# Output projection of a DeltaNet/mLSTM block on one core: two equal seven-product DeltaNet blocks, the last 512 mLSTM columns behind them, and two 512-column mLSTM blocks in the DeltaNet drain

## The chip, the core and the metric

One Trainium2 chip, one of its cores. The time is that of one launch, in microseconds (us) on the device. The kernel before was run three times: 2253.58, 2257.16 and 2258.36, median 2257.16. The profile is of one further execution, which took 2254.1 us. Engines are named as in the profile: PE is TensorE (PEld its weight loads), DVE VectorE, ACT ScalarE, POOL GpSimd, SP SyncE, which issues DMAs. `SPq` and `ACTq` are the queues in which SyncE and ScalarE issue DMAs.

## The reference

One decoder block on 512 rows of 2048 columns, in float32:

```python
u = _rmsnorm(h, norm_w)
proj = jnp.matmul(u, w_in.astype(jnp.float32))
...
h_a = h_a * jax.nn.sigmoid(ml_o) * jax.nn.silu(ml_z)     # mLSTM branch, 512 x 2048
...
h_b = _merge_heads(h_b) * jax.nn.silu(dn_z)              # DeltaNet branch, 512 x 2048
...
y_a = jnp.matmul(h_a, w_out[:ML_WIDTH])
y_b = jnp.matmul(h_b, w_out[ML_WIDTH:])
return jax.nn.sigmoid(gate_a) * y_a + jax.nn.sigmoid(gate_b) * y_b
```

`h + y` then passes a final RMSNorm with the weight `final_norm_w`. The change touches only the last part: the two products with `w_out`, the gates, the residual and the final norm.

## The kernel before, in words

**Number format.** A float32 operand is split into a high part `hi` (ScalarE, `split_hi`, L135) and the rest `lo` (VectorE, `split_lo`, L138). Every product of two tiles is three matmuls: hi x hi, hi x lo, lo x hi. One row tile is P = 128 rows; NC = 4 of them make the 512 rows. KT = 16 tiles of 128 make the 2048 of the inner dimension, KH = 8 pairs of them. NO = 512 is a wide column block, NB = 256 a narrow one.

**Order of the work.** TensorE runs its instructions in the order in which the program writes them. The side work is made of generators: `start(gen, wait)` puts one on the list `active`, and each `tick()`, called between groups of matmuls, advances those that are due, so that their instructions are written at that place. For the engines other than TensorE a list scheduler orders what has been written, by priority: `urgent(n)` and `tc.high_priority` move an instruction ahead, `behind(eng)` puts it after the newest weight split on that engine ("A" ScalarE, "V" VectorE). Weight tiles pass one ring, `wr` of NRAW = 4 slots, and `wh`, `wl` of NSPL = 4 slots each; `plan` lists them in the order of use, and `prepare` loads up to RAHEAD = 4 and splits up to SAHEAD = 3 tiles ahead of the one in use. Other tiles use `wr` slots too: gate tiles `ty`, h tiles `hr`, and the `b21` below. Tiles of one tag get their slots in the order in which the program allocates them; a pool that is opened after another was closed gets its memory when the last use of the closed pool's tiles is over.

**Drain.** The last DeltaNet chains (dn_back, dn_chain, travel) run as generators beside four narrow mLSTM output blocks (loop from L1281; `proj_tm`, 16 ticks each): block b computes columns 256 b to 256 b + 255 of `h_a @ w_out[:2048]`, gates them with `tgn`, adds half of that to x and stores y_d. After each block `close()` (L1268) looks whether `active` is empty; if so it closes the drain's pools (wks, with the pool wk), opens the pool sb2 (ring `wr3` of three slots, scratch `t13` of one buffer, `s4`, `X2`) and sa2 (`su`), and starts `h_sums`.

**h sums.** `h_sums` (from L1237) loads the eight pairs of DeltaNet h tiles (`hs`, in `wr3`), forms four sums per pair into a `t13` tile (`hsum`, L1256 to L1259) and splits them with `split_scaled` (L1217 on ScalarE, L1218 on VectorE). They are the left operands of the seven products.

**Wide mLSTM blocks** (loop from L1521): columns 1024 to 1535 (nb = 2) and 1536 to 2047 (nb = 3), 192 matmuls of 512 columns each, 12 per k tile and two ticks per k tile. At the end of a block four gated evacuations (L1568), then the generator `store_y`: for each row tile a load of x, the operation of L1538 with `behind("V")`, a store to y_d. Beside the second one run `load_h` (DeltaNet h, split into `uh`, `ul` over the mLSTM h) and, from its tick 22, `lead`: three loads of quads and the preparation of the first.

**DeltaNet output.** `seven_stage` computes `h_b @ w_out[2048:]` in two blocks of 1024 columns (c1 and c2 = c1 + 512) by seven products in place of eight, on halves of the inner dimension, rows and columns. A *quad* is one pair of k tiles: three 256 KB loads into `wr3` (L527), sums of weights (`prep_sums`, L550, L551, L562) and splits (`prep_sums`, `prep_pair`). Group A has 4 products of 8 quads (192 matmuls), B has 3 (144). A stores its sum `ts` to DRAM (t2_d), and B reads it back. `sink_y` holds what the finished products turn into: gate tiles `ty` (L1316), gated (L1321), added to y_d by an accumulating GpSimd DMA.

**The last of the two blocks is special** (`final_y`, from L1356): its group B is cut into 24 single pieces, its own loads `b21` (L513) take `wr` slots, GpSimd subtracts eight times (L554) and issues the stores, and the final norm is written into a table `beside` by piece: reading y_d back (`known`), gates (`times`, L1399), additions (`plus`, L1406), squares (L1410), the norm weight (`weigh`, L1421, GpSimd), the factor (L1426 to L1428) and the scaled output (by_act L1432, by_dve L1438 and L1440). KLAST = 4 pieces are done row tile by row tile at the end.

Of the kernel before, what the change touches and what calls it, by code (L numbers as in the profile page):

```python
# [15 lines left out]
P = 128  # L16
S = 512
# [10 lines left out]
YNARROW = 4  # L28
# [3 lines left out]
KLAST = 4  # L32
# [23 lines left out]
def hybrid_body(  # L56
# [95 lines left out]
    plan += [("n", b * NB, k) for b in range(YNARROW) for k in range(0, KT, KP)]  # L152
    plan += [("o", nb * NO, k) for nb in range(YNARROW * NB // NO, D // NO) for k in range(KT)]
# [4 lines left out]
    def load_raw():  # L158
        kind, c, k = plan[len(raws)]
        if kind == "m":  # L160

            qk = w_in[k * P:(k + KP) * P, ML_Q:ML_V].rearrange("(k p) (a n) -> p k a n", p=P, a=2)[:, :, :, c * P:(c + 1) * P]
            src, nk, n = None, KP, NB
        elif kind in "in":
            src, nk, n = (w_in if kind == "i" else w_out)[k * P:(k + KP) * P, c:c + NB], KP, NB
        else:
            src, nk, n = w_out[k * P:(k + 1) * P, c:c + NO], 1, NO
# [89 lines left out]

    def proj_tm(col0, kind="i"):
        ps = [psj.tile([P, 2, NB], F32, tag="pj", name="pjt") for _ in range(2)]
        for kt0 in range(0, KT, KP):  # L260
            hi, lo = next_w(kind, col0, kt0)
            for c in range(NC):
                for k in range(KP):
                    kt = kt0 + k
                    o = ps[c // 2][:, c % 2, :]
                    tsl = slice(c * P, (c + 1) * P)
                    T.matmul(o, uh[:, kt, tsl], hi[:, k, :], start=(kt == 0 and c % 2 == 0), stop=False,
                             skip_group_check=True)
                    T.matmul(o, uh[:, kt, tsl], lo[:, k, :], start=False, stop=False, skip_group_check=True)
                    T.matmul(o, ul[:, kt, tsl], hi[:, k, :], start=False, stop=(kt == KT - 1),  # L270
                             skip_group_check=True)
                if c % 2:
                    tick()
        return ps

# [218 lines left out]
    def seven_stage(sbp, su, s4, X, t2_d, w_, k0, blocks, sinks, hook, final=None):  # L494
# [5 lines left out]
                 for g in ("A" if final and b == len(blocks) - 1 else "AB") for i in range(KH)]  # L500
        rawq, partq, b21 = [], {}, {}

        def in_final(b):
            return final is not None and b == len(blocks) - 1

        def load_b21(q):

            if q < len(quads) and in_final(quads[q][3]):
                _, c1, c2, b, g, i = quads[q]
                k2 = slice((k0 + 2 * i + 1) * P, (k0 + 2 * i + 2) * P)  # L510
                with tc.high_priority(offset=2 * PRIO):
                    b21[q] = wp.tile([P, NO], F32, tag="wr", name="b21", bufs=NRAW)
                    nc.sync.dma_start(b21[q], w_[k2, c1:c1 + NO])  # L513
# [25 lines left out]
        def prep_sums(q):  # L539
# [5 lines left out]
            with tc.high_priority(offset=2 * PRIO):  # L545
                ts = wp.tile([P, 1, NO], F32, tag="tg", name="ts", bufs=3)
                if g == "A":
# [5 lines left out]
                    if in_final(b):  # L553
                        G.tensor_tensor(out=b21[q], in0=b21[q], in1=ts[:, 0, :], op=ALU.subtract)  # L554
                        G.dma_start(t2_d[b % 2, i], b21[q])
                        load_b21(q + 1)
                    else:
                        nc.scalar.dma_start(t2_d[b % 2, i], ts[:, 0, :])
# [30 lines left out]
        def seven(n0, kind, c1, c2):  # L589
# [5 lines left out]
            if in_final(n0 // (2 * KH)):  # L595
                fin = final(c1, c2, m1, m5, m7, LHS["B"], split, t2_d[(n0 // (2 * KH)) % 2])
# [14 lines left out]
            if in_final(n0 // (2 * KH)):  # L611
                for n in range(KH - 2):
                    prep_sums(n0 + n + 1)
# [991 lines left out]
```

## Time and profile before

| | us |
|---|---|
| median of the runs (3) | 2257.16 (2253.58 to 2258.36) |
| the profiled execution | 2254.1 |
| its span, in which all instructions lie | 2252.3 |
| TensorE busy | 2171.1 (96%) |
| VectorE busy | 1699.0 (75%) |
| ScalarE busy | 956.4 (42%) |
| GpSimd busy | 298.6 (13%) |
| granted TensorE clock, mean | 0.99 |

The profile is one execution. A view groups instructions by line, engine, operation and tile; `L604` is line 604 of the kernel, `out<-in` the tiles by the program's names, `x16` a count. Times on a timeline count from the start of the span. In a waits view, `A <- B: 6.0, 1, 6.0` means that instruction A's engine stood idle for 6.0 us, once, 6.0 at most, and that B ended last. "PEclk" is the granted TensorE clock as a share of full speed. A busy share over the whole span mixes stages with different limits; what follows looks at the last 410 us alone.

### The profile page before, as it was taken

To read this page: it belongs to the slowest core of one execution; us is meant where nothing else is said; L and a number is where in the kernel's file an instruction comes from. 1 tells how busy PE (TensorE), PEld (TensorE's weight loads), DVE (VectorE), ACT (ScalarE), POOL (GpSimd) and SP (SyncE) were. 2 spreads that over 40 slices of the span, in tenths; PEclk is the share of its full clock that TensorE was granted. 3 is DMA by queue.
4 is the path that set the end of the run, shared out by engine and by line. 5 is a ranking of instruction groups with operands and counts; after the bars stand their busy time and mean duration, and the time that the engine had idled before them with its cause. 6 is when DMAs were issued, how large, how long until landed. Compare 5 with 4: busy or idle time off the path is not lost. (4 is left out here: it accounts for less than half of the span.)

```text
span 2252.3 us, 32412 instructions
## 1 busy us (share of the span) xinstructions
PE 2171.1 (96%) x10976; PEld 1797.4 (80%) x10976; DVE 1699.0 (75%) x2953; ACT 956.4 (42%) x1834; POOL 298.6 (13%) x362
## 2 busy tenths in 40 slices
PE   7999999999999999999999999999999998999986
PEld 5878778778788888888878887888888888987765
DVE  5788788778877777876789877777767685477777
ACT  5444444445444443444443433443444443243334
POOL 0320000000000000000322522222222211000124
PEclk9999999999999999999999999999999999999998
DMA  5456666667666776685776865767566665588686
GB/s 159 134 164 199 203 191 211 205 192 231 213 215 213 236 227 183 221 260 182 185 180 165 194 154 141 161 157 160 144 157 150 160 171 166 153 264 257 208 238 243
DMA packets 536264, 430.61 MB, mean 191 GB/s; under 512 B 241697, under 2 KB 403714, under 8 KB 536098
## 3 DMA queue, kind: packets, MB, share of 16 engines
q1 hardware_dynamic: 435682, 361.35, 56.7%
q10 hardware_dynamic: 98624, 63.00, 8.9%
q0 software_dynamic: 1792, 4.20, 0.9%
q8 instruction: 86, 1.41, 0.3%
q14 instruction: 80, 0.66, 0.1%
HBM read 340.27 MB, written 88.15 MB: 190 GB/s over the span
## 5 line engine op out<-in xcount | busy, mean ns | idle before, releaser
L135 ACT CAST wh<-wr 128x512 fp32r<-128x512 f32 (+1 forms) x560 | 389.9, 698 | 524.9 <-PE pj L253 244.8
L138 DVE TENSOR_TENSOR wl<-wr,wh 128x512 fp32r<-128x512 f32 (+1 forms) x560 | 470.0, 842 | 154.2 <-ACT wh L135 145.4
L252 PE MATMUL pj<-uh,wh 128*128 128x512 f32 x1024 | 428.6, 419 | 2.8 <-ACT yp L816 2.8
L254 PE MATMUL pj<-uh,wl 128*128 128x512 f32 x1024 | 400.8, 391 | 0.0
L253 PE MATMUL pj<-ul,wh 128*128 128x512 f32 x1024 | 399.9, 391 | 0.0
L605 PE MATMUL ps<-wl,uh 128*128 128x512 f32 x640 | 252.4, 394 | 5.8 <-DVE wl L138 5.7
L604 PE MATMUL ps<-wh,uh 128*128 128x512 f32 x640 | 251.2, 393 | 5.8 <-DVE X L664 4.1
L606 PE MATMUL ps<-wh,ul 128*128 128x512 f32 x640 | 249.8, 390 | 0.0
L135 ACT CAST wh<-t 128x1024 fp32r<-128x1024 f32 x112 | 117.9, 1053 | 267.4 <-PE ps L606 116.6
L135 ACT CAST wh<-ts 128x512 fp32r<-128x512 f32 x216 | 133.3, 617 | 231.0 <-DVE ts L562 180.8
L254 PEld LDWEIGHTS pj<-uh,wl 128*128 128x128 f32 x1024 | 192.5, 188 | 43.1
L605 PE MATMUL ps<-wl,suh 128*128 128x512 f32 x576 | 224.5, 390 | 1.7 <-DVE wl L138 1.7
L604 PE MATMUL ps<-wh,suh 128*128 128x512 f32 x576 | 224.8, 390 | 0.9 <-ACT qk L363 0.5
L606 PE MATMUL ps<-wh,sul 128*128 128x512 f32 x576 | 224.4, 390 | 0.0
L252 PEld LDWEIGHTS pj<-uh,wh 128*128 128x128 f32 x1024 | 193.5, 189 | 37.7 <-ACT yp L816 3.2
L253 PEld LDWEIGHTS pj<-ul,wh 128*128 128x128 f32 x1024 | 193.5, 189 | 32.8
L138 DVE TENSOR_TENSOR wl<-t,wh 128x1024 fp32r<-128x1024 f32 x112 | 141.0, 1259 | 50.3 <-ACT wh L135 49.8
L138 DVE TENSOR_TENSOR wl<-ts,wh 128x512 fp32r<-128x512 f32 x216 | 151.1, 703 | 33.6 <-ACT wh L135 33.6
L605 PEld LDWEIGHTS ps<-wl,uh 128*128 128x128 f32 x640 | 120.6, 188 | 39.0 <-DVE wl L138 15.1
L604 PEld LDWEIGHTS ps<-wh,uh 128*128 128x128 f32 x640 | 120.7, 189 | 35.9 <-DVE X L664 8.9
L550 DVE TENSOR_TENSOR t<-wr 128x1024 f32<-128x1024 f32 x112 | 137.2, 1225 | 7.4 <-DMA wr<-in_w_in_dram 6.9
L562 DVE TENSOR_TENSOR ts<-wr 128x512 f32<-128x512 f32 x104 | 71.7, 690 | 92.8 <-DMA wr<-t_d 73.9
(320 smaller groups left out, 3714.3 us busy)
## 6 DMA issues: line engine op xcount, KB each, us to landing
wr<-in_w_in_dram SPq DMA_DIRECT2D x704, 256.0 KB, 3.7
wr<-in_w_out_dram SPq DMA_DIRECT2D x144, 256.0 KB, 4.3
t_d<-ts ACTq DMA_DIRECT2D x96, 256.0 KB, 4.1
wr<-t_d SPq DMA_DIRECT2D x96, 256.0 KB, 4.0
wr<-in_w_in_dram SPq DMA_DIRECT2D x64, 128.0 KB, 2.9
xt<-in_x_dram SPq DMA_DIRECT2D x8, 512.0 KB, 7.1
tg_d<-X ACTq DMA_DIRECT2D x16, 256.0 KB, 5.5
tg_d<-to ACTq DMA_DIRECT2D x16, 256.0 KB, 5.0
```

The source lines that it names most:

```text
L135: newest["A"] = A.copy(hi, src).ins
L138: newest["V"] = V.tensor_tensor(out=lo, in0=src, in1=hi.bitcast(F32), op=ALU.subtract).ins
L252: T.matmul(ps[j], hi[:, k, wsl], uh[:, kt, :], start=(kt == 0), stop=False)
L253: T.matmul(ps[j], hi[:, k, wsl], ul[:, kt, :], start=False, stop=False)
L254: T.matmul(ps[j], lo[:, k, wsl], uh[:, kt, :], start=False, stop=(kt == KT - 1))
L550: V.tensor_tensor(out=t13, in0=r[:, 1:3, :], in1=r[:, 0:2, :], op=ALU.subtract)
L562: V.tensor_tensor(out=ts[:, 0, :], in0=r[:, 0, :], in1=r[:, 2, :], op=ALU.subtract)
L604: T.matmul(ps[t], ah, hi, start=(g == "A" and i == 0), stop=False, skip_group_check=True)
L605: T.matmul(ps[t], ah, lo, start=False, stop=False, skip_group_check=True)
L606: T.matmul(ps[t], al, hi, start=False, stop=(i == KH - 1), skip_group_check=True)
```

## The change

1. **Drain.** The four narrow blocks (YNARROW = 4, `proj_tm`, plan kind "n") are gone. In their place `wide_block` computes columns 0 to 511 and 512 to 1023 (YDRAIN = 2), with three pj banks and one wk bank each and with gate tiles `tgs` in the drain's pool wk (tags "ke" and "vn"). `close()` is called after each k tile. A third call of `wide_block` computes columns 1024 to 1535, with `load_h`, `lead` and gate tiles in X2, as the old second wide block did for the last columns.
2. **DeltaNet output.** Both blocks of 1024 columns now run the same two groups. `final_y`, the parts of `seven_stage` that serve it, `b21` and GpSimd's subtractions are gone. The last block's sink is `sink_last`: it closes the pool of `su` once group A is over, opens a pool with hf, fw and jk, adds the gated products to hf on GpSimd (`plus`) after reading y_d and x into hf (`known`), and starts `load_hm`.
3. **The last 512 mLSTM columns** (1536 to 2047) come behind them as `last_block`. `load_hm` loads the mLSTM h again, k tile by k tile, into a ring of its own ("hmr", three slots) and splits it over the DeltaNet h during group B and the block itself, in the order LAST (even k tiles first). The weights of the last KLAST = 6 k tiles have slots in `wr3`, `w2` and the ring; they are multiplied row tile by row tile, and behind each row tile stands `done_c`: gate, residual, square, factor, scaling, store. Squares (ScalarE) and `weigh` (GpSimd) of the first 1536 columns run beside the block.

The diff, cut to its core (the removed `final_y` and `proj_tm` are left out):

```diff
-YNARROW = 4
+YDRAIN = 2
...
-KLAST = 4
+KLAST = 6
...
-    plan += [("n", b * NB, k) for b in range(YNARROW) for k in range(0, KT, KP)]
-    plan += [("o", nb * NO, k) for nb in range(YNARROW * NB // NO, D // NO) for k in range(KT)]
+    plan += [("o", nb * NO, k) for nb in range(D // NO - 1) for k in range(KT)]
+    nlast = len(plan)
+    LAST = [k for o in range(2) for k in range(o, KT, 2)]
+    plan += [("o", D - NO, k) for k in LAST[:KT - KLAST]]
...
-        limit[0] = len(plan)
+        limit[0] = nlast
...
-                    if in_final(b):
-                        G.tensor_tensor(out=b21[q], in0=b21[q], in1=ts[:, 0, :], op=ALU.subtract)
-                        G.dma_start(t2_d[b % 2, i], b21[q])
-                        load_b21(q + 1)
-                    else:
-                        nc.scalar.dma_start(t2_d[b % 2, i], ts[:, 0, :])
+                    nc.scalar.dma_start(t2_d[b % 2, i], ts[:, 0, :])
...
+    def wide_block(nb, pools, tgs, then=()):
+
+        sl = slice(nb * NO, (nb + 1) * NO)
+        ps = [pool.tile([P, NO], F32, tag=t, name="py") for pool, t in pools]
...
+        start(load_tg(), 18)
+        for gen, wait in then:
+            start(gen, wait)
+        ks = range(KT)
+        for kt in ks[:KT - KTAIL]:
+            w = wide_w(nb * NO, kt)
+            for c in range(NC):
+                products(ps, kt, c, *w, ks)
+                if c % 2:
+                    tick()
+            if nb < YDRAIN:
+                close()
+        ws = [(kt, wide_w(nb * NO, kt)) for kt in ks[KT - KTAIL:]]
+        for c in range(NC):
+            for kt, w in ws:
+                products(ps, kt, c, *w, ks)
+            tick()
+            with urgent(3):
+                V.scalar_tensor_tensor(out=tgs[c], in0=tgs[c], scalar=1.0, in1=ps[c], op0=ALU.add, op1=ALU.mult)
+        start(store_y(), 1)
+
+    for b in range(YDRAIN):
+        wide_block(b, ((psj, "pj"),) * 3 + ((psw, "wk"),),
+                   [wk.tile([P, NO], F32, tag=("ke", "vn")[c // 2], name="tgy", bufs=4) for c in range(NC)])
     while "sb" not in late:
         tick()
         close()
...
+            start(load_hm(), 3)
...
+            if len(raws_) < KT:
+                with behind("A"):
+                    load(nc.scalar)
...
+    def hook_y():
+        limit[0] = len(plan)
+        prepare(used[0] - 1)
...
+        def beside():
...
+            for c in range(NC):
+                nc.sync.dma_start(tgs[c], tg_d[c, :, nsl])
+                for n, a in enumerate(range(0, CT, NO)):
+                    square(c, a, a + NO, n)
+                weigh(c, 0, HD)
+                yield 1
+                weigh(c, HD, CT)
+                yield 2
+
+        def done_c(c):
+            o, r = hf[:, c, nsl], rf[:, c:c + 1]
+            with urgent(3 + c):
+                V.scalar_tensor_tensor(out=tgs[c], in0=tgs[c], scalar=1.0, in1=ps[c], op0=ALU.add, op1=ALU.mult)
+                V.scalar_tensor_tensor(out=o, in0=tgs[c], scalar=0.5, in1=o, op0=ALU.mult, op1=ALU.add)
+            square(c, CT, D, 3, False)
...
+            G.tensor_scalar(out=hf[:, c, HD:CT], in0=hf[:, c, HD:CT], scalar1=r, scalar2=None, op0=ALU.mult)
...
+        start(beside(), 3)
+        start(load_tail(), 2)
+        start(split_tail(), 2 * (KT - KLAST) - 8)
+        for kt in ks[:KT - KLAST]:
...
+        for c in range(NC):
+            for n, kt in enumerate(tail):
...
+                products(ps, kt, c, *tw[kt], ks)
+                if n % 2:
+                    tick()
+            done_c(c)
+
+    wide_block(YDRAIN, banks[1], [X2[:, c // 2, c % 2, :] for c in range(NC)],
+               [(load_h(h_d, lambda k: 32, 2, True), 4), (lead(), 2 * KT - 10)])
     for b, blk in enumerate(OUTS):
         seven(2 * KH * b, *blk)
+    last_block()
+    while active:
+        tick()
```

427 lines of the change are left out of this document (166 added, 261 removed).

## The prediction, made before the result was known

> **What bounds the kernel now.** I read first the table by stage: the stretch from the first mLSTM output block to the end, cut where the program goes from one block to the next. Columns are the stretch in us, its length, busy time of each engine (with instructions), the granted TensorE clock, DMA share and GB/s.
>
> ```profile
> core 0: us, PE busy (x) PEld busy (x) DVE busy (x) ACT busy (x) POOL busy (x), PEclk, DMA share, GB/s
> 1843.10:1963.90 120.80, 111.97 (x965) 110.19 (x965) 66.72 (x143) 38.98 (x93) 10.31 (x12) 0.94 0.59 165
> 1963.90:2007.50 43.60, 43.60 (x195) 36.09 (x194) 31.68 (x62) 18.48 (x30) 0.00 (x0) 1.00 0.85 280
> 2007.50:2055.10 47.60, 44.90 (x193) 35.68 (x192) 31.60 (x50) 18.60 (x31) 0.00 (x0) 1.00 0.78 230
> 2055.10:2100.40 45.30, 44.02 (x193) 35.88 (x192) 36.68 (x50) 18.98 (x29) 0.00 (x0) 1.00 0.75 250
> 2100.40:2136.60 36.20, 34.20 (x145) 26.62 (x144) 27.14 (x35) 12.89 (x16) 6.00 (x6) 1.00 0.67 205
> 2136.60:2195.60 59.00, 48.74 (x194) 38.31 (x194) 45.76 (x51) 18.19 (x27) 17.85 (x19) 0.91 0.83 239
> 2195.60:2241.20 45.60, 38.52 (x145) 29.24 (x143) 36.23 (x42) 23.16 (x44) 22.13 (x12) 0.89 0.70 249
> 2241.20:2252.30 11.10, 0.04 (x1) 0.00 (x0) 4.03 (x10) 3.02 (x4) 1.27 (x2) 0.72 0.51 208
> ```
>
> Row by row: four narrow mLSTM blocks in the DeltaNet drain; two wide blocks; group A (192 matmuls) and group B (144) of the first DeltaNet block; A and B of the last one; the tail. The second row is the measure: 192 matmuls without an idle moment take 43.6 us, 0.227 us each, so a whole DeltaNet block (336) is worth 76.4 us. The first block takes 45.3 + 36.2 = 81.5, the last 59.0 + 45.6 = 104.6 with the clock at 0.91 and 0.89. TensorE bounds everything but those last 28 us of loss and the tail.
>
> The waits and SyncE's timeline say what the largest hole is:
>
> ```profile
> PE ps L604 <- DVE ty L1321: 6.0, 1, 6.0
> DVE ty L1321 <- DMA ty<-tg_d: 5.5, 1, 5.5
> ```
> ```profile
> 2138.23 0.33 SPq L1316 DMA_DIRECT2D ty<-tg_d  x1
> 2142.08 4.53 SPq L513 DMA_DIRECT2D b<-in_w_out_dram  x3
> ```
>
> A gate tile was issued only at 2138.2, because the special block's own loads (L513, name b21) hold slots of the same ring of four; TensorE stood 6.0 us. The clock pays too:
>
> ```profile
> 2140.20:2146.20 6.00, 0.01 (x1) 0.00 (x0) 0.73 (x2) 1.03 (x2) 0.00 (x0) 0.79 0.99 205
> 2146.20:2150.50 4.30, 4.29 (x10) 3.42 (x11) 4.30 (x5) 0.00 (x0) 2.73 (x3) 0.50 0.72 170
> ```
>
> After 6.0 us without matmuls, 4.3 us at half clock: 2.2 us more lost.
>
> **The change, part by part.** I sum against the profiled execution (span 2252.3, time 2254.1) and put the difference on the median of 2257.16.
>
> *1. Four narrow blocks become two wide ones in the drain.* The same columns, 768 matmuls of 256 columns against 384 of 512.
>
> ```profile
> 1960.19 0.28 PE L270 MATMUL pjt<-wh,ul 128*128 128x256 f32 x1
> 1960.31 0.28 PE L267 MATMUL pjt<-wh,uh 128*128 128x256 f32 x1
> ```
>
> Starts are 0.12 us apart, so 768 x 0.120 = 92.2 becomes 384 x 0.227 = 87.2: **-5.0**. The drain's DeltaNet matmuls and their ticks stay (32 ticks per wide block, 64 in all, as before). The first wide block needs three pj banks at once, so it waits for the second copy of the last projection too:
>
> ```profile
> 1847.24 0.59 ACT L816 COPY yp<-pj 128x512 f32<-128x512 f32 x1 [3.06 <-DMA h_d<-to]
> ...
> 1848.35 0.57 ACT L816 COPY yp<-pj 128x512 f32<-128x512 f32 x1
> ```
>
> The second ends 1.1 us after the first: **+1.1**. The block also keeps one wk bank of three; each of the two DeltaNet chains has one wk tile alive at a time, so I cost that at nothing (up to 3 us if an evacuation is late). Drain: 116.9 instead of 120.8.
>
> *2. When the DeltaNet sums can start.* This decides. `close()` releases the drain's pool wks and opens sb2 in its place, with the ring (wr3), the scratch (t13) and, above it, su. It now stands behind every k tile of the drain's blocks. Count the drain's ticks: dn_back starts at 25 and ends at 32, the second dn_chain runs from 35 to 57, its travel at 60. The stores that it issues are the end of the drain in the trace:
>
> ```profile
> L852 ACTq DMA_DIRECT2D h_d<-to x8: 310/508/592, 1955.8 to 1959.9; - x8
> ```
>
> Tick 60 is the last tick of the second wide block's loop (32 + 28), so `close()` succeeds there, four ticks before that block ends. But the block's gate tiles tgs are now tiles of wk ("ke", "vn"), and the pool that follows gets its memory only after their last use: the four operations of store_y, at ticks up to 20 of the next block, the last one queued behind the split of k tile 12. The nearest row is the same operation in the block of before that also loads the DeltaNet h:
>
> ```profile
> 2040.78 0.69 DVE L138 TENSOR_TENSOR wl<-wr,wh 128x512 fp32r<-128x512 f32 x1
> 2041.38 0.68 DVE L1538 SCALAR_TENSOR_TENSOR xn<-X,xn 128x512 f32<-128x512 f32 x1
> ```
>
> It ends 2042.06 - 2007.50 = 34.6 us into its block. The lower bound: split 12 needs the slot of k tile 8, so 9 x 12 x 0.227 = 24.5, and some 2 us for the two splits and the operation: 26.5. I take **33**, near the row, since the ring of weights that delays it is loaded alike. Then come loads and sums, one tile pair after another since t13 has one buffer:
>
> ```profile
> hs<-h_d SPq DMA_DIRECT2D x16, 256.0 KB, 4.3
> ```
> ```profile
> 1975.52 0.42 DVE L1256 TENSOR_TENSOR hsum<-hs 128x256 f32<-128x256 f32 x1
> ...
> 1978.60 0.48 DVE L1218 SCALAR_TENSOR_TENSOR t4l<-hsum,normc,t4h 128x256 fp32r<-128x256 f32 x1
> ...
> 1987.66 0.41 DVE L1256 TENSOR_TENSOR hsum<-hs 128x256 f32<-128x256 f32 x1
> ```
>
> Three pairs in 12.1 us, 4.04 us each, with one weight split between; a pair itself takes 3.6. The tiles of t13 are given out in program order: the first quad's comes behind the seventh pair's (lead starts at tick 22, prepares at 28; the pairs stand at ticks 2, 6, ... 26). So the first quad is prepared from 33 + 4.4 + 6 x 4.04 + 3.6 = 65.2, and its first product needs
>
> ```profile
> L550 DVE TENSOR_TENSOR t<-wr 128x1024 f32<-128x1024 f32 x16 | 19.5, 1216 | 0.3 <-DMA wr<-in_w_out_dram 0.2
> L551 DVE TENSOR_TENSOR ts<-wr,t 128x512 f32<-128x512 f32 x16 | 11.0, 690 | 1.5 <-DMA t2o_d<-ts 0.8
> L135 ACT CAST wh<-ts 128x512 fp32r<-128x512 f32 x24 | 14.8, 616 | 22.0 <-DVE ts L562 14.2 <-DVE ts L551 7.7
> ```
>
> and a 0.69 split: 3.2, with handovers 3.5. TensorE starts the DeltaNet output 68.7 us after the third wide block began; in before the block took 47.6 (third row). **+21.1**. In before this work was ready early (h sums ran beside the first wide block, from 1975.5). Bounds: 62 and 72.
>
> *3. First DeltaNet block:* 81.5. The wait for the gated evacuation at its start (1.3) is gone, half clock after the wait costs 2.2 (row above), and the second quad's t13 comes behind the eighth pair: ready 8.8 us after the first, when TensorE needs 5.5 + 2.2 = 7.7, so 1.1. Sum **+2.0**, 83.5.
>
> The Trainium skill ("TensorE: Matmul & The Clock Gate", Part 1) says that a window of about 3.4 us idle halves the clock until TensorE was busy for such a window. An estimate by it is 1.7 us here, whatever the length of the wait; the sum would be 0.5 lower. The row agrees in kind, with 4.3 us.
>
> *4. Second DeltaNet block, now like the first.* b21, the eight GpSimd subtractions and the 24 single pieces go; the gate tile of the 6.0 us wait finds its slot. It has company instead in group B: 6 of the 16 h splits, 6 additions on GpSimd. VectorE then has per quad of 4.1 us 2.6 (0.69 + 0.69 + 1.22) + 0.75, and GpSimd's time comes on top:
>
> ```profile
> 2216.00 5.48 DVE L138 TENSOR_TENSOR wl<-wr,wh 128x512 fp32r<-128x512 f32 x2
> ```
> ```profile
> 2215.28 5.65 POOL L1421 TENSOR_TENSOR hf<-hf,fw 128x1024 f32<-128x1024 f32 x2
> ```
>
> A split of 0.69 took 2.7 while GpSimd multiplied. I take 81.5 + 3.5 = 85.0 in place of 104.6: **-19.6** (bounds 78 and 95).
>
> *5. The last wide block* goes from ahead (43.6, which had no loss) to the end: 43.6 + loss. In it stand 10 h splits, 13 weight splits, 12 squares and this on GpSimd:
>
> ```profile
> L1421 POOL TENSOR_TENSOR hf<-hf,fw 128x1024 f32<-128x1024 f32 x4 | 10.8, 2718 | 0.6 <-ACT jkf L1410 0.6
> L1406 POOL TENSOR_TENSOR hf<-hf,ty 128x512 f32<-128x512 f32 x4 | 6.4, 1603 | 25.3 <-DVE ty L1399 25.3
> L1421 POOL TENSOR_TENSOR hf<-hf,fw 128x512 f32<-128x512 f32 x2 | 3.5, 1772 | 0.0
> ```
> ```profile
> L1218 DVE SCALAR_TENSOR_TENSOR ul<-hr,normc,uh 128x512 fp32r<-128x512 f32 x8 | 6.0, 748 | 9.2 <-ACT uh L1217 9.2
> ```
>
> Splits are three tiles (8 us) ahead and the six tail tiles are prepared early, so only what is left when the first row tile reaches its tail can be late: some six VectorE operations at 2.3 instead of 0.7 in the 14 us after GpSimd begins. I take 4 late and 1.5 of clock: **+5.5** (bounds 0 and 14.5). The waits of ScalarE's and SyncE's queues behind squares and loads are in that bound.
>
> *6. Tail.* The chain behind the last matmul keeps its members; the other rows' work is further ahead (4.1 us per row tile instead of 2.7), and GpSimd takes 512 of the 1024 columns that VectorE scales at the end (L1438, L1440). 11.1 becomes 10.8: **-0.3** (bounds -1.2 and +1).
>
> Sum: -3.9 + 21.1 + 2.0 - 19.6 + 5.5 - 0.3 = +4.8. Forecast 2257.2 + 4.8 = **2262 us**.
>
> **The rivals.** *Opened in time:* if sb2 opens within some 11 us of the third block's begin (`close()` one tick late falls to the loop that issues store_y at once, or the pools do not wait so), the first quad is ready by 47.6 and 21.1 + 3.3 go: -20, 2238 us. For it: the pairs stood finished long before in the trace. Against it: the count of ticks, exact to one. *GpSimd and VectorE exclude each other through the last block:* 10.9 + 7.1 + 6.4 = 24.4 on GpSimd (four of each row), and VectorE needs 13 x 0.69 + 8 x 0.75 + 9 x 0.69 = 21.2 before the first row tile ends its tail at 0.227 x (10 x 12 + 18) = 31.3: 14.2 late, 8.7 over the sum, 2271 us. It decides from 10 us of overlap upwards. For it: the 5.48 row; against it: splits go first and are ahead.
>
> The Trainium skill ("GPSIMD Engine Reference", Key points) says that GpSimd shares its SBUF interfaces with VectorE's two-input instructions; by that rule this rival holds for every split. The 5.48 row agrees.
>
> *It does not do what it says:* the second block keeps half of its 28 us, because VectorE (45.8 of 59.0 busy) and not b21 held it: +10.6, 2272 us.
>
> **How the numbers follow.** Late opening as summed 0.55, own range 2254 to 2271; opened in time 0.23; exclusion 0.14; no cure 0.05; anything else 0.03. A measurement of this kernel tells 0.2%, 4.5 us, from no change. The forecast's case gives 0.03 faster, 0.22 same, 0.30 slower; with the others 0.28, 0.23, 0.49. The range 2236 to 2273 takes in most of the first rival and the lower half of the next two: some 0.8.
>
> **What would show it.** Right: in the changed trace the first h sums come some 35 us after the third wide block's start, TensorE idles some 20 us before the first DeltaNet product, with a half clock behind; the second DeltaNet block takes some 85 us; the narrow lines' 92 us are gone. Wrong: h sums beside the third block's first tiles, no such gap, and a time under 2245; or TensorE's waits in the last block's tail are over 10 us with long VectorE splits under GpSimd multiplications.

## The result, and the profile after

The changed kernel took 2259.86 us (median of 12 runs, 2249.73 to 2263.19); the kernel before, run beside it, 2257.00 (12 runs). The ratio is 1.0006, with a 95% interval of 0.9993 to 1.0019: no difference that these runs can tell. The forecast was 2262, in the range of 2236 to 2273; its +4.8 us lies just above the interval, which is -1.6 to +4.3 us.

The profiled execution took 2260.2 us, span 2258.4. Below is its table by stage, with the columns of the table of before. The rows: the two wide blocks in the drain; the third wide block; the stretch from its last matmul to the first DeltaNet product; groups A and B of the first DeltaNet block; A and B of the second; the last wide block; the tail.

```profile
core 0: us, PE busy (x) PEld busy (x) DVE busy (x) ACT busy (x) POOL busy (x), PEclk, DMA share, GB/s
1847.30:1957.90 110.60, 103.58 (x581) 85.09 (x580) 63.08 (x138) 38.71 (x92) 10.74 (x12) 0.98 0.61 170
1957.90:2001.70 43.80, 43.80 (x193) 35.80 (x192) 25.00 (x44) 16.66 (x29) 0.00 (x0) 1.00 0.79 238
2001.70:2026.20 24.50, 0.20 (x1) 0.02 (x1) 21.64 (x41) 11.28 (x18) 0.00 (x0) 0.59 0.74 229
2026.20:2074.60 48.40, 47.59 (x192) 37.85 (x193) 42.50 (x57) 20.13 (x30) 0.00 (x0) 0.93 0.74 241
2074.60:2108.70 34.10, 33.41 (x145) 26.79 (x144) 25.56 (x34) 12.57 (x16) 3.68 (x4) 1.00 0.72 215
2108.70:2158.80 50.10, 46.27 (x193) 36.88 (x193) 38.37 (x49) 18.10 (x26) 3.46 (x4) 0.97 0.84 241
2158.80:2197.90 39.10, 35.17 (x145) 27.81 (x144) 27.76 (x35) 16.90 (x24) 4.91 (x3) 0.96 1.01 366
2197.90:2244.70 46.80, 44.19 (x193) 35.70 (x191) 35.70 (x44) 24.04 (x51) 29.48 (x17) 1.00 0.38 121
2244.70:2258.40 13.70, 0.12 (x1) 0.00 (x0) 4.47 (x10) 4.59 (x7) 7.75 (x5) 0.63 0.56 230
```

The third row is the one to see: for 24.5 us TensorE does nothing while VectorE is busy for 21.6 of them. This wait before the first DeltaNet product is called the hole below. Against it stand the drain (120.8 before) and the special block that is gone (104.6 before, now 89.2). The sixth and seventh rows show what replaced that block's loss: in group B the DMA engines are full (1.01, 366 GB/s; before, that block's two rows had 0.83 and 0.70).

From the first output matmul to the end, before took 2252.3 - 1843.1 = 409.2 us and the changed kernel 2258.4 - 1847.3 = 411.1: +1.9. The other 4.2 us by which the spans differ lie ahead of it, in code that is the same in both: over the 13 profiles of this study the first output matmul comes at 1841.1 to 1850.6 us. So profiles are compared below by their output stage alone, and a stage that an edit leaves alone still varies by some us from execution to execution (group A of the second block, in the nine other kernels that keep it: 43.5 to 49.7).

Term by term, forecast and measured (us, output stage of the two profiles):

| step of the prediction | forecast | measured | worked out |
|---|---|---|---|
| 1 drain | -3.9 | -10.2 | 110.6 - 120.8 |
| 2 late sums | +21.1 | +20.7 | 68.3 - 47.6 |
| 3 first DeltaNet block | +2.0 | +1.0 | 48.4 + 34.1 - 81.5 |
| 4 second DeltaNet block | -19.6 | -15.4 | 50.1 + 39.1 - 104.6 |
| 5 last wide block | +5.5 | +3.2 | 46.8 - 43.6 |
| 6 tail | -0.3 | +2.6 | 13.7 - 11.1 |
| sum | +4.8 | +1.9 | |

Step 2 can be followed on the timelines (start, length, engine and line; lines of the changed kernel). First VectorE's and SyncE's queues at the end of the second drain block's `store_y` (L1249 is its operation), then VectorE and TensorE at the first product:

```profile
1985.40 0.69 DVE L1249 SCALAR_TENSOR_TENSOR xn<-tgy,xn 128x512 f32<-128x512 f32 x1
```
```profile
1986.17 0.38 SPq L1160 DMA_DIRECT2D hs<-h_d  x1
```
```profile
2023.29 1.22 DVE L521 TENSOR_TENSOR t<-wr 128x1024 f32<-128x1024 f32 x1
```
```profile
2026.21 0.77 PE L568 MATMUL ps<-wh,tuh 128*128 128x512 f32 x1 [24.31 <-issue]
```

The last use of a gate tile in the closed pool ends at 1986.1, and 0.1 us later SyncE issues the first load of h tiles for the sums (`hs`): 28.2 us after the third block began. Seven pairs later, in the next free slot of VectorE, the first quad's subtraction starts at 2023.29. The mechanism is the forecast one; the page names no releaser for the 24.31 us ("issue"), and the wait has to be followed through VectorE by hand. In its last 14 us nothing but the chain is left: the sums of pairs four to seven and the quad start 3.55 us apart (2009.10, 2012.65, 2016.20, 2019.75, 2023.29).

### The profile page after: what moved, and what is told of

It is laid out like the page before. It is cut to its first block, busy times and chain, and to the rows that moved or that the text cites. A ratio compares the mean times of both kernels' runs of the same rounds, so it can differ in the third digit from the quotient of the medians.

```text
span 2258.4 us, 31622 instructions
## 1 busy us (share of the span) xinstructions
PE 2160.7 (96%) x10592; PEld 1770.6 (78%) x10592; DVE 1706.3 (76%) x2963; ACT 967.3 (43%) x1850; POOL 295.7 (13%) x356
## 4 chain that ended last, share of the span: by engine, by line
PE 64%; DMA 14%; DVE 11%; issue 4%; ACT 2%; SPq 2%; POOL 1%; ACTq 0%; DVEq 0%; POOLq 0%
PE ps L569 9%; PE ps L570 9%; PE ps L568 9%; PE pj L254 8%; PE pj L255 8%; PE pj L256 8%; DVE wl L138 5%; DMA wr<-t_d 4%; DMA wr<-in_w_out_dram 3%; DMA wr<-in_w_in_dram 2%; PE py L1226 2%; PE py L1227 2%; PE py L1228 2%; ACT wh L135 2%; SPq L498 1%
## 5 line engine op out<-in xcount | busy, mean ns | idle before, releaser
L135 ACT CAST wh<-wr 128x512 fp32r<-128x512 f32 (+1 forms) x538 | 379.7, 708 | 496.6 <-PE pj L255 252.1
L138 DVE TENSOR_TENSOR wl<-wr,wh 128x512 fp32r<-128x512 f32 (+1 forms) x538 | 451.6, 843 | 142.6 <-ACT wh L135 136.0
L569 PE MATMUL ps<-wl,uh 128*128 128x512 f32 x672 | 266.4, 396 | 8.2 <-DVE wl L138 8.0
L568 PE MATMUL ps<-wh,uh 128*128 128x512 f32 x672 | 264.8, 394 | 5.4 <-DVE X L610 2.9
L570 PE MATMUL ps<-wh,ul 128*128 128x512 f32 x672 | 263.3, 392 | 0.0
L135 ACT CAST wh<-ts 128x512 fp32r<-128x512 f32 x224 | 138.0, 617 | 242.6 <-DVE ts L528 188.6
L256 PEld LDWEIGHTS pj<-uh,wl 128*128 128x128 f32 x1024 | 192.7, 188 | 43.1
L138 DVE TENSOR_TENSOR wl<-t,wh 128x1024 fp32r<-128x1024 f32 x112 | 137.1, 1224 | 48.4 <-ACT wh L135 47.7
L569 PEld LDWEIGHTS ps<-wl,uh 128*128 128x128 f32 x672 | 127.0, 189 | 44.4 <-DVE wl L138 19.1
L568 PEld LDWEIGHTS ps<-wh,uh 128*128 128x128 f32 x672 | 126.8, 189 | 39.0 <-DVE X L610 9.3
L528 DVE TENSOR_TENSOR ts<-wr 128x512 f32<-128x512 f32 x112 | 77.8, 694 | 101.1 <-DMA wr<-t_d 77.2
L570 PEld LDWEIGHTS ps<-wh,ul 128*128 128x128 f32 x672 | 127.1, 189 | 25.5
```

The costliest lines, as they stand in the source:

```text
L135: newest["A"] = A.copy(hi, src).ins
L138: newest["V"] = V.tensor_tensor(out=lo, in0=src, in1=hi.bitcast(F32), op=ALU.subtract).ins
L256: T.matmul(ps[j], lo[:, k, wsl], uh[:, kt, :], start=False, stop=(kt == KT - 1))
L528: V.tensor_tensor(out=ts[:, 0, :], in0=r[:, 0, :], in1=r[:, 2, :], op=ALU.subtract)
L568: T.matmul(ps[t], ah, hi, start=(g == "A" and i == 0), stop=False, skip_group_check=True)
L569: T.matmul(ps[t], ah, lo, start=False, stop=False, skip_group_check=True)
```

## The experiments

All times of runs, beside the kernel before on the same chip; "output stage" is the profiled execution from its first output matmul to the end. The runs were made on several chips, where the kernel before had medians of 2257.0 to 2263.6, so compare rows by the ratio and not by the median. e3 and e10 have one run each and no ratio.

| run | median us (runs) | ratio to before, 95% | output stage us |
|---|---|---|---|
| before | | 1 | 409.2 |
| changed kernel | 2259.86 (12) | 1.0006 (0.9993 to 1.0019) | 411.1 |
| e1_store_at_once | 2248.52 (5) | 0.9950 (0.9937 to 0.9964) | 405.6 |
| e2_drain_alone | 2248.03 (6) | 0.9947 (0.9934 to 0.9960) | 402.8 |
| e3_no_reload | 2248.81 (1) | | 404.3 |
| e4_last_store_sp | 2259.07 (12) | 0.9999 (0.9985 to 1.0014) | 415.4 |
| e5_tail_vector | 2256.68 (7) | 0.9972 (0.9960 to 0.9984) | 406.8 |
| e6_odd_later | 2247.38 (6) | 0.9933 (0.9920 to 0.9946) | 397.8 |
| e7_both | 2241.75 (4) | 0.9909 (0.9895 to 0.9922) | 393.2 |
| e8_b21_later | 2247.21 (6) | 0.9932 (0.9919 to 0.9944) | 396.8 |
| e9_all | 2240.30 (6) | 0.9911 (0.9893 to 0.9929) | 395.2 |
| e10_reload_unsplit | 2253.47 (1) | | 406.0 |
| e11_odd_sooner | 2237.63 (4) | 0.9883 (0.9867 to 0.9900) | 393.6 |

**e1: open the pool early.** At the end of `wide_block`:

```diff
-        start(store_y(), 1)
+        if nb == YDRAIN - 1:
+            for _ in store_y():
+                pass
+        else:
+            start(store_y(), 1)
```

> The changed kernel with one difference: behind the second wide drain block, store_y is written at once instead of as a generator of 20 ticks, so the last use of a tile of the closed pool wk should lie some 6 to 9 us into the third wide block instead of 28.1. Theory (the late opening of sb2 makes the 24.5 us hole before the first DeltaNet product): the first load of DeltaNet h tiles for the sums moves to about 8 us into the block, and the hole goes; but VectorE was busy 25.0 + 21.6 = 46.6 us until the first product, and the block has 43.8, so some 3 to 8 us of the hole stay: about -18 us, 2242 where the changed kernel has 2260. Rival A (the pools do not wait for this use, something else opens late): the hole stays at 24 us and the time at 2260. Rival B (VectorE's work alone makes the hole): the sums start early, but the hole stays over 15 us, time 2252 or more.

SyncE's queue, and e1's third wide block up to the first product:

```profile
1969.88 1.64 SPq L1160 DMA_DIRECT2D hs<-h_d  x3
```
```profile
1958.60:2021.30 62.70, 46.83 (x194) 36.85 (x192) 45.93 (x84) 28.11 (x47) 0.00 (x0) 0.92 0.85 256
```

The first `hs` load moved from 28.2 to 11.3 us into the block, so the pool's last use was what held it: rival A is out. But an opening 16.9 us earlier brought the first product only 5.6 us earlier (62.7 after the block's begin instead of 68.3). The hole shrank from 24.5 to 11.9, and inside the block TensorE now waited another 4.1 us for weight splits. They were late for two reasons. The longest wait (2.5 us) ends with a split that stood behind the splits of sums in ScalarE's queue, and then 0.5 us for its weights to land; the next (1.0 us) ends with one for which ScalarE stood 2.1 us for the weights alone:

```profile
2003.28 0.62 ACT L135 CAST wh<-wr 128x512 fp32r<-128x512 f32 x1 [2.12 <-DMA wr<-in_w_out_dram]
```

Theory and rival B are both half true. VectorE had 45.9 us of work until the first product, in a block of 43.6, and the chain of pairs stretched: their sums start 4.3 to 11.0 us apart instead of 3.55, with h splits, weight splits and evacuations between. The output stage is 5.5 us shorter and the runs gained some 12 us; the profiled execution was the slowest of e1's five (2252.84), 4.3 above the median, and how much of the difference that is stays open.

**e2: the drain alone.** The kernel before with `YNARROW`'s loop and `proj_tm` replaced by

```diff
+    plan += [("o", nb * NO, k) for nb in range(D // NO) for k in range(KT)]
...
+    for b in range(YDRAIN):
+        wide_block(b, ((psj, "pj"),) * 3 + ((psw, "wk"),),
+                   [wk.tile([P, NO], F32, tag=("ke", "vn")[c // 2], name="tgy", bufs=4) for c in range(NC)])
```

> The kernel before with the two wide drain blocks alone (same wide_block, gate tiles in wk); the rest of the output stage as before. Theory: the drain takes 110.6 us as in the changed kernel instead of 120.8, and the late opening costs nothing here since two wide blocks (87 us) follow before the first DeltaNet product: about -10 us, 2247 where the kernel before has 2257. By the step as forecast (-3.9 for the drain) 2253. Rival (the late opening delays the sums by 28 us and the DeltaNet blocks wait here too): 2257 or more, with a hole before the first product.

e2's drain and its two wide blocks:

```profile
1841.60:1954.30 112.70, 106.36 (x582) 87.42 (x581) 63.38 (x139) 39.03 (x93) 10.37 (x12) 0.95 0.61 168
1954.30:1997.80 43.50, 43.50 (x194) 36.05 (x193) 21.86 (x39) 13.24 (x22) 0.00 (x0) 1.00 0.70 220
1997.80:2049.20 51.40, 47.91 (x194) 37.69 (x193) 43.08 (x77) 26.62 (x45) 0.00 (x0) 0.93 0.92 283
```

The drain took 8.1 us less than before (10.2 in the changed kernel) and not 3.9. The output stage is 6.4 us shorter in this profile; the runs gave 12.0 (0.40 to 0.66%), and the difference is not attributed. The rival is out, since the DeltaNet blocks do not wait here, but the late opening is not free: with sums, h splits and quads pressed into the second wide block, VectorE is busy 43.1 of its 51.4 us and the block is 3.8 us longer than in before (47.6). The first DeltaNet block took 43.5 + 35.9 instead of 81.5.

**e3 and e10: what the reload costs.** e3 leaves out `load_hm` (loads and splits of the mLSTM h for the last block), e10 leaves out the splits alone; both then multiply the DeltaNet h in the last block.

```diff
-            start(load_hm(), 3)
```
```diff
-            split_hm(k, raws_[n])
```

> The changed kernel without load_hm: the second load of the mLSTM h tiles (16 of 256 KB) and their 16 splits are left out, so the last wide block multiplies the DeltaNet h that is still in uh and ul. Theory (in group B of the second DeltaNet block the loads for later work fill the DMA engines, share 1.01, and its quads land late): group B takes about 35 us instead of 39.1 and the last wide block 44 to 45 instead of 46.7; group A (50.1) stays, since nothing of load_hm runs beside it. Rival (VectorE's splits for the reload, not the transfers, hold group B): the same shorter B, but with VectorE's waits for quads (3.4 us at L528) unchanged.

> The changed kernel with the second load of the mLSTM h tiles kept but their 16 splits left out (nothing reads the loaded tiles; the last wide block multiplies the DeltaNet h that is still in uh and ul). It tells the transfers from the splits in what load_hm costs group B of the second DeltaNet block: 39.1 us in the changed kernel, 35.9 in e3_no_reload without both. If the transfers hold it: 38.5 or more; if ScalarE's and VectorE's splits do: 36.5 or less.

Group B of the second DeltaNet block, the last wide block and the tail, first of e3, then of e10:

```profile
2157.00:2192.90 35.90, 33.84 (x146) 26.72 (x145) 25.70 (x33) 14.44 (x20) 6.00 (x4) 1.00 0.96 358
2192.90:2236.40 43.50, 43.50 (x193) 35.82 (x191) 23.16 (x34) 18.56 (x42) 27.45 (x18) 1.00 0.26 91
2236.40:2247.00 10.60, 0.15 (x1) 0.00 (x0) 3.36 (x6) 3.02 (x4) 4.81 (x4) 0.70 0.54 223
```
```profile
2155.50:2197.20 41.70, 37.28 (x145) 28.52 (x144) 25.64 (x34) 13.98 (x19) 6.16 (x4) 0.92 1.00 355
2197.20:2240.70 43.50, 43.50 (x193) 35.88 (x191) 21.79 (x32) 18.87 (x42) 26.81 (x16) 1.00 0.45 143
2240.70:2251.40 10.70, 0.19 (x1) 0.00 (x0) 3.38 (x6) 3.02 (x4) 4.82 (x4) 0.63 0.54 222
```

This tells the two apart. With the transfers and without the splits group B takes 41.7 us, without both 35.9: the transfers hold it. (In the eight kernels that keep both it takes 39.1 to 43.0, and e10 lies among them.) All three run at nearly the same rate (366, 358 and 355 GB/s) and move 14.33, 12.86 and 14.79 MB. e3's 35.9 is also what group B of the first block takes (34.1 in the changed kernel, 36.2 in before), so there TensorE's own work may set the length. No cost of the splits shows in group B, but 3.3 us in the last block (46.8 against 43.5) and 3.0 in the tail (13.7 against 10.7). Block and tail together take 54.1 and 54.2 us without the splits, and 58.7 to 60.5 in the four profiles that keep both as in the changed kernel, so the price is 4.5 to 6.4.

**e4 and e5: the tail.** e4 issues the last store of a row tile from SyncE. e5 does so too, and takes `weigh` of columns 1024 to 1535 and their scaling from GpSimd:

```diff
-            nc.scalar.dma_start(out[c * P:(c + 1) * P, HD:D], hf[:, c, HD:D])
+            nc.sync.dma_start(out[c * P:(c + 1) * P, HD:D], hf[:, c, HD:D])
```
```diff
-                weigh(c, HD, CT)
...
-            G.tensor_scalar(out=hf[:, c, HD:CT], in0=hf[:, c, HD:CT], scalar1=r, scalar2=None, op0=ALU.mult)
             with urgent(2):
-                V.scalar_tensor_tensor(out=o, in0=o, scalar=r, in1=fw[:, nsl], op0=ALU.mult, op1=ALU.mult)
+                V.scalar_tensor_tensor(out=hf[:, c, HD:D], in0=hf[:, c, HD:D], scalar=r, in1=fw[:, HD:D], op0=ALU.mult, op1=ALU.mult)
```

> The changed kernel with the second store of each row tile in done_c issued by SyncE instead of ScalarE. Theory: in the tail ScalarE's queue stands at that store until GpSimd has scaled its 512 columns (2.1 to 2.6 us), and the next row tile's square is queued behind it, which makes each of the last row tiles cost 4.4 us: without it about 3.3 us per row tile, tail 10.5 instead of 13.7, time -3. Rival (GpSimd's own chain of factor and scaling, 0.6 + 2.1 to 2.6 us per row tile, sets the pace): tail within 1 us of 13.7.

> The changed kernel with GpSimd relieved in the last wide block: columns 1024 to 1535 are no longer multiplied by the norm weight on GpSimd beside the block (4 of 1.7 us) nor scaled there in done_c (4 of 2.1 to 2.6 us); instead one VectorE operation per row tile scales and weighs columns 1024 to 2047, and the store behind it is issued by SyncE. Theory (the tail of 13.7 us is long because GpSimd's queue still multiplies when the first row tile asks for its factor, 3.7 us late, and each later row tile follows in a serial chain of about 4 us): the first factor comes on time, tail 9 to 10 instead of 13.7, last block 45 to 46 instead of 46.7, time about -4.5, 2255 beside 2260. Rival (the chain from evacuation over square and factor to the scaling is the whole tail): tail stays over 12.5, time within 2 us of 2260.

The theory behind e4 fell: the tail took 13.4, the time did not move. (Its output stage is 4.3 us longer than the changed kernel's; that lies in stages that the edit leaves alone.) The rival's chain on GpSimd is not it either, since GpSimd stood idle for 1.16 us before each of the last three factors, until VectorE had the sum. What sets the pace is the order of VectorE's queue. In e4 (L1508 scales a row tile, L1496 evacuates the next one):

```profile
2245.40 0.15 DVE L1501 TENSOR_SCALAR bia<-bia 128x1 f32<-128x1 f32 x1
2246.24 0.75 DVE L1508 SCALAR_TENSOR_TENSOR hf<-hf,bia,fw 128x512 f32<-128x512 f32 x1 [0.69 <-POOL bia L1502]
2246.91 0.68 DVE L1496 SCALAR_TENSOR_TENSOR X<-X,py 128x512 f32<-128x512 f32 x1
...
2249.35 0.15 DVE L1501 TENSOR_SCALAR bia<-bia 128x1 f32<-128x1 f32 x1
```

The evacuation stands behind the scaling, the scaling behind the factor, the factor behind the former square: one loop of 3.95 us per row tile, in which each member waits for the one before. In the changed kernel ScalarE's queue was a member too: the factors start 4.51, 3.29 and 4.44 us apart, 12.24 in all, and in e4 11.87, so taking the store away let the loop through VectorE show and gained 0.4. The loop starts late, as GpSimd's queue in the changed kernel shows, beside VectorE's:

```profile
2229.51 9.82 POOL L1355 TENSOR_TENSOR hf<-hf,fw 128x512 f32<-128x512 f32 x5
2239.29 0.57 POOL L1502 TENSOR_TENSOR bia<-bia,mhalf 128x1 f32<-128x1 f32 x1
```
```profile
2227.20 2.89 DVE L1164 SCALAR_TENSOR_TENSOR ul<-hmr,normc,uh 128x512 fp32r<-128x512 f32 x1
...
2235.62 0.15 DVE L1501 TENSOR_SCALAR bia<-bia 128x1 f32<-128x1 f32 x1
```

The first row tile's sum was ready at 2235.8, and GpSimd was multiplying by the norm weight until 2239.3. In e5 its factor came 1.0 us after the sum and not 3.5; the tail took 11.7 (expected 9 to 10, the rival over 12.5), the last block 44.6, and the output stage 4.3 us less, as expected. The runs gained more, some 7.7 us (the ratio fell from 1.0006 to 0.9972). A loop of some 4.5 us per row tile stayed.

**e6: less of VectorE's work in the third block.** e1, with the odd h tiles (used from group B on) split later and the fourth x tile of `store_y` in the weight ring:

```diff
-               [(load_h(h_d, lambda k: 32, 2, True), 4), (lead(), 2 * KT - 10)])
+               [(load_h(h_d, lambda k: 32, 4, True, range(0, KT, 2)), 4), (lead(), 2 * KT - 10)])
+    start(load_h(h_d, lambda k: 32, 4, True, range(1, KT, 2)), 12)
```

> The kernel of the run e1_store_at_once with the odd DeltaNet h tiles (needed by group B alone) loaded and split beside the first DeltaNet block's group A instead of the third wide block (8 loads of 256 KB, 8 VectorE operations of 0.75 us), the even ones every four ticks, and the fourth x tile of store_y in the weight ring. Theory (with the pool open, the 11.9 us that stay of the hole are VectorE's work: 45.9 us busy of 62.7): sb2 opens some 8 us into the block instead of 11.3, VectorE's work before the first product falls by 6, hole 2 to 6 us, group A 48 to 50: time about -6 beside e1, 2242. Rival (the serial chain of sums through the one t13 buffer sets the hole, not VectorE's load): the hole falls by the 3 us of the earlier opening alone, time -2 or less.

```profile
1962.40:2013.70 51.30, 43.68 (x193) 35.86 (x191) 42.59 (x80) 25.55 (x44) 0.00 (x0) 0.97 0.92 289
2013.70:2063.50 49.80, 47.23 (x193) 37.86 (x194) 44.13 (x59) 20.71 (x31) 0.00 (x0) 0.93 0.76 248
```

The first product came 51.3 us into the block instead of 62.7, while the pool opened 4.6 us into it instead of 11.3: 11.4 us for 6.7. The chain from the first pair's sums to the first quad took 35.8 us instead of 43.5, so what stood between the pairs had stretched it, and t13 alone does not set the hole. The edit takes loads out of the weight ring as well as splits out of VectorE's queue, though, and the two were not tried apart: the loss inside the block is gone (7.3 of the 11.4 us) and the hole fell from 11.9 to 7.8, where the theory had 2 to 6. The runs gained less than this profile: 0.9933 after 0.9950, with overlapping intervals.

**e7, e9, e11: together.** e7 is e6 with e5's tail. In e9 the odd splits are tied behind the newest weight split, and a row tile's scaling behind the next evacuation:

```diff
+                if len(ks) < KT and k % 2:
+                    e.enter_context(behind("A"))
+                    e.enter_context(behind("V"))
...
+            if c:
+                finish(c - 1, e)
```

(`finish` scales and stores a row tile, `e` is the next one's second evacuating operation.) e11 is e9 with `load_h(h_d, lambda k: 32, 3, True, range(1, KT, 2)), 2`, so that the odd tiles come sooner.

> The two former edits together (e6_odd_later with the tail of e5_tail_vector): if the stages are independent the sum of both, about 2238; if the hole's gain is given back in the second DeltaNet block or the last one, 2243 or more.

> The kernel of the run e7_both with two more edits: the odd h splits are tied behind the newest weight split (in e7 three of them stood ahead of the first quad's operations in VectorE's queue, while TensorE waited), and a row tile's final scaling on VectorE is put behind the next row tile's evacuation (in e7 the evacuation stood behind it, which made a serial chain of 4.47 us per row tile). Theory: the hole before the first DeltaNet product falls from 8.4 to some 5.5 us, the tail from 12.9 to about 9.5: together -6, 2236 beside e7's 2242. Rival (both orders cost nothing, since the sums and the factor's chain end last): within 2 us of 2242.

> The kernel of the run e9_all with the odd h tiles started at tick 2 of group A, one every 3 ticks, instead of tick 12 and every 4. In e9 the last two of them were loaded only at 2083.8 and 2087.8, in group B, behind gate tiles that hold the weight ring until their accumulation has landed, and group B took 42.9 us instead of 35.9. Theory: with all eight loaded before the gate tiles come, group B is back at 34 to 36, group A stays at 50 to 52: about -5, 2235 beside e9's 2240. Rival (VectorE's added work in group A takes it all): A grows to 55 or more, time within 2 us of 2240.

e7's 0.9909 (0.9895 to 0.9922) takes in the sum of the two edits (0.9899), so no gain is seen to be given back. Its VectorE, in the hole:

```profile
2006.23 0.75 DVE L1164 SCALAR_TENSOR_TENSOR ul<-hr,normc,uh 128x512 fp32r<-128x512 f32 x1 [0.81 <-ACT uh L1163]
2006.90 1.22 DVE L521 TENSOR_TENSOR t<-wr 128x1024 f32<-128x1024 f32 x1
2008.04 0.74 DVE L1164 SCALAR_TENSOR_TENSOR ul<-hr,normc,uh 128x512 fp32r<-128x512 f32 x1
...
2009.89 0.68 DVE L522 TENSOR_TENSOR ts<-wr,t 128x512 f32<-128x512 f32 x1
```

Splits that group B alone needs stand between the first quad's operations. e9 cured that (hole 8.4 to 5.0), and the tail fell from 12.9 to 11.1, but last block and tail together only from 56.7 to 56.2. Its time is e7's, as its rival had it, but for another reason: two tied h tiles were loaded only in group B, behind gate tiles that hold the ring, and B took 42.9 us instead of 35.9. SyncE and its wait in e9, then groups A and B, the last block and the tail of e11:

```profile
2083.75 4.43 SPq L1160 DMA_DIRECT2D hr<-h_d  x2
SPq L1160 <- DMA y_d<-ty: 6.9, 2, 3.6
```
```profile
2005.60:2060.30 54.70, 48.16 (x193) 36.55 (x193) 47.34 (x64) 25.13 (x39) 0.00 (x0) 0.96 0.77 248
2060.30:2095.50 35.20, 34.22 (x144) 26.73 (x145) 26.46 (x35) 12.25 (x17) 3.67 (x4) 1.00 0.70 214
...
2183.50:2227.10 43.60, 43.60 (x193) 35.85 (x192) 32.36 (x43) 25.26 (x53) 19.43 (x11) 1.00 0.44 141
2227.10:2237.10 10.00, 0.12 (x1) 0.00 (x0) 4.08 (x6) 2.63 (x4) 0.55 (x1) 0.75 0.59 243
```

In e11 group B is back at 35.2, and 2.6 of the gain goes to group A (54.7 after 52.1), where VectorE is now busy 47.3 us. With 0.9883 (0.9867 to 0.9900) it is 1.2% faster than the kernel before and has the lowest ratio of this study; the last block runs without loss and the tail takes 10.0. Its interval still touches those of e7 and e9, and its output stage is as long as e7's (393.6 and 393.2), so its lead over e7 is not shown.

**e8: the ring conflict alone.** e2 with the first `b21` load moved from three quads ahead into `prep_sums`:

```diff
-                if n == N - 3 and n0 + N + 1 < len(quads) and in_final(quads[n0 + N][3]):
-                    load_b21(n0 + N)
...
+                        if q not in b21:
+                            load_b21(q)
```

> The kernel of the run e2_drain_alone (before with the wide drain) with the first load of b21 written where its sum is prepared, behind the gate tiles of the first DeltaNet block, instead of three quads before the block's end. Theory (b21 holds the slot that the last gate tile needs, which makes the 5.9 us wait and the half clock behind it): the wait goes, the special last block falls from 104.7 to some 97, time -7 beside e2, 2241. Rival (SyncE's queue or the DMA share makes the gate tile late, not the slot): the wait stays within 2 us, time within 2 us of e2's 2248.

TensorE's longest wait in the DeltaNet output of e2, with what SyncE waited for just before it issued that gate tile (at 2128.98), and then TensorE's waits of e8:

```profile
PE ps L603 <- DVE ty L1353: 5.7, 1, 5.7
SPq L1348 <- DMA t2o_d<-b: 2.1, 1, 2.1
```
```profile
PE ps L606 <- DVE wl L138: 6.7, 4, 3.8
```

In e2 the gate tile was issued only when a b21 tile had been stored, and with b21 loaded later the wait is gone, so the slot caused it. But waits of 6.7 for weight splits, one of them 3.8, came in its place (2.4 in e2), the special block fell from 104.6 to 100.9 only (expected 97), and the runs do not tell e8 from e2 (0.9932 and 0.9947). Of the block's 28 us of loss, removing the ring conflict gave back 4, not the 8 that the wait and its half clock had cost.

## Why the prediction was right, and where its steps were not

The forecast's case is what happened: the pool opened late, TensorE stood for 24.5 us before the first DeltaNet product, and e1 shows the mechanism on the chip. That the sum came within 3 us of the output stage is partly luck: -6.3, -0.4, -1.0, +4.2, -2.3 and +2.9 cancel. The +4.8 itself is not confirmed; the runs tell no difference.

*Step 1, the drain, was mis-sized:* -3.9 against -10.2. The count of matmuls was right (-5.0). Added to it as unchanged were the waits and their half clock, and those fell too. TensorE's waits, of before and after:

```profile
PE pjt L267 <- ACT yp L816: 3.1, 1, 3.1
PE pqk L953 <- DVE kq L826: 2.7, 1, 2.7
PE pw L1044 <- DVE tb L1014: 2.6, 1, 2.6
```
```profile
PE py L1226 <- ACT yp L762: 3.9, 1, 3.9
PE pqk L899 <- DVE kq L772: 3.2, 1, 3.2
```

The wait for the third pj bank grew by 0.8 (forecast 1.1), and the third wait is gone. TensorE's idle time fell from 8.8 to 7.0, and its busy time by 8.4 where the cadence explains 5.0: the rest is clock, 0.98 after 0.94. But that part varies between executions: in the twelve profiles that have this drain it took 110.6 to 114.0 us, and in e11 (114.0, clock 0.94) 6.8 less than in before, of which 5.2 are busy time. Against the one profile of before the step was short by 3 to 6 us. Which of the wide blocks' properties removed the third wait was not tried.

*Step 2 was right in its sum and wrong in both of its terms.* The opening came at 28.2 us, not 33, near the lower bound worked out from the splits (26.5); the seven pairs and the first quad took 37.1 us from there to the quad's subtraction and not 32.2, because the first pair's sums began 7.3 us after the load was issued (4.4 counted) and one pair, with five h splits and four evacuations in VectorE's queue, took 7.8 us for 4.04; the others kept to 3.55 to 4.0. The prediction took the pairs as a chain by their own pace, and never added up what else VectorE has to do in the block. That error hardly shows in the forecast, but it does in the first rival: "opened in time" was priced at 24 us below the forecast, and e1, which opens at the 11 us named there, measured about 12 below the changed kernel.

*Step 3* held in its sum, 82.5 after 83.5, with group A 3.1 longer than before and B 2.1 shorter. *Step 4* was mis-sized by 4.2. All of it is in group A, 50.1 where the prediction took the first block's 45.3; the other kernels that keep it had 43.5 to 49.7, so this is partly the one execution, and it was not taken apart further. By the prediction's own measure of 76.4 us the block still lost 12.8 of its 28.2, so the rival "it does not do what it says" is nearer than its 0.05 (its price does not follow, either: half of 28.2 on top of 76.4 is 90.5, or +5.5). Its cause is not shown: TensorE's waits there are for weight splits, 5.9 us on VectorE and 1.8 on ScalarE, and what made those of group A late was not tried. Group B came as forecast (39.1 for 36.2 + 3.5), but for another cause than VectorE under GpSimd: its transfers held it (e3 and e10). The changed kernel's DMA view of that stretch:

```profile
DMA packets 9529, 14.33 MB, mean 366 GB/s; under 512 B 756, under 2 KB 4340, under 8 KB 9398
```
```profile
wr<-in_w_out_dram SPq DMA_DIRECT2D x13, 256.0 KB, 6.1
```

14.3 MB in 39.1 us, and weights that landed after 3.9 us over the whole span need 6.1 here. The prediction counted that group's instructions, and none of its bytes. The Trainium skill ("Perfetto Trace Analysis", Roofline) says that a single core's 16 DMA engines bound it at about 435 GB/s together; the trace agrees in kind, with a mean of 366 and a share of 1.01.

*Step 5* was in its bounds (3.2 for 5.5), and the rival "GpSimd and VectorE exclude each other" did not decide: VectorE's operations beside GpSimd's did stretch (2.89 us in the row above, for 0.75), but splits were ahead, and TensorE waited 2.6 us in the block. *Step 6* failed: the tail grew by 2.6 instead of shrinking. It took the other rows' work to be further ahead, but the row tiles follow in one loop, and that loop began late: the first factor waited 3.5 us behind GpSimd's multiplications, which had themselves been late behind ScalarE's squares and h splits (without the splits, in e10, the first factor starts 0.1 us after its sum, and the tail is 10.7). The prediction named ScalarE's queue as a bound of step 5 and did not carry it into the tail.

The rule of the Trainium skill on the clock ("TensorE: Matmul & The Clock Gate", Part 1) was put at 1.7 us for the wait before the first product. The granted clock there:

```profile
2026.20:2030.00 3.80, 3.26 (x7) 2.28 (x8) 3.29 (x7) 1.34 (x3) 0.00 (x0) 0.50 0.38 132
2030.00:2033.10 3.10, 3.10 (x9) 2.42 (x8) 2.96 (x4) 0.76 (x3) 0.00 (x0) 0.50 0.84 274
2033.10:2036.00 2.90, 2.90 (x13) 2.16 (x13) 2.50 (x4) 1.77 (x3) 0.00 (x0) 0.98 0.94 342
```

Half clock for 6.9 us, 3.4 lost, with one wait of 0.5 us within; the row of before (4.3 us) was the nearer guess of the two, and both were low. It differs from execution to execution: in e10, at the same place, the clock was 0.50 for 3.5 us and 0.81 on average over the next 3.4, which loses 2.4.

## What to carry to other kernels

A tile of a closed pool holds up everything that the next pool is to hold until its last use, so look for the last reader of what a pool is closed over. When a wait is priced by a chain of operations, also count what else stands in the queue between its members: here the pairs ran 3.55 us apart when VectorE had nothing else, and 4.3 to 11.0 apart beside the block, so an opening 16.9 us earlier brought the first product only 5.6 us sooner. Work that is moved to follow other work takes its bytes along, and here the stretch whose DMA share rose from 0.7 to 1.0 was set by its transfers.

## What the runs showed that was not expected

Between executions, the code ahead of the output stage, the same in all 13 profiles, ended anywhere from 1841.1 to 1850.6 us; what varies there was not looked into. With its DMA engines full, group B of the second block ran at 355 to 366 GB/s in three kernels with different mixes of loads. Moving the store to another queue (e4) gained 0.4 us in the tail, although the queue did stand at it: a loop through VectorE of nearly the same length was waiting behind it.
